# Naming each place of a tile pool: the plan, not the pool, says which place a tile takes

## The chip, the cores and the metric

The kernel runs on one core of a Trainium2 chip. The metric is the time of one execution on the device in microseconds (us); lower is better. The core's engines are TensorE (PE; its weight loads are shown as PEld), VectorE (DVE), ScalarE (ACT), GpSimd (POOL) and SyncE (SP), which issues nearly all transfers. Each runs its own instructions in the order in which they stand, and waits on semaphores for the others.

## The reference

One mixer layer on x of 2048 tokens by 1024 channels: RMS norm, one input projection (2816 columns), two groups of heads side by side (retention in chunks of 128, sliding-window attention of 128 with sinks), gates, one output projection, and x added.

```python
h = rms_norm(x, norm_w).astype(x.dtype)
proj = jnp.einsum('bsd,de->bse', h, w_in).astype(jnp.float32)
rq, rk, rv, rg, sq, sk, sv, sg = jnp.split(proj, offsets, axis=-1)
ro = retention(rotary(rq), rotary(rk), rv)        # scores * decay, state over chunks
ro = group_norm(ro) * ret_norm_w * jax.nn.silu(rg)
so = sliding_window_attention(sq, sk, sv, q_norm_w, k_norm_w, sinks, rel_bias)
so = so * jax.nn.silu(sg)
mixed = jnp.concatenate([ro, so], axis=-1)
x = x + jnp.einsum('bse,ed->bsd', mixed, w_out)
```

## The kernel before, in words

The projections are four products of 2048 tokens, each done as seven half-size products (W2 with its blocks B2, then W1, W3 and W4 in `layer`) over eight pairs of token chunks. Every operand is split into a high and a low part (`split`: ScalarE writes the high part, VectorE the low part), and three matmuls per block multiply the parts. That is the group acc<-w,x of the profile. Sums of blocks (x, w, s, t, u, r) are made on VectorE. Between the products run the window attention (`window`), the retention (`retention`) and the gates (`gate`); their matmuls write tiles named m. What must live longer than SBUF allows goes to DRAM and comes back: sums of blocks to s_dram, projections to aq_dram, rq_dram and g_dram, head outputs to ro_dram and so_dram. Tiles that are transposed by a transfer are first copied by ScalarE (tile apart), stored to planes_dram and read back turned (`turn_by_dma`).

No operation is issued where it is written. `op` records it with what it reads (`r`), writes (`w`) and holds (`also`), a due time and a cost per engine. `Program.emit` then lists them all: at each step it looks at the operations that are ready on every engine, takes the one that can start first by its own clock, allocates its new tiles and issues it. So the source has one line, L421, for all instructions of the profile, and the order on each engine is the plan's. `Order.put` fixes that order for the framework below, which adds the semaphore waits by itself: an instruction that writes a tile waits until the last reader of the tile that lay in the same place has ended.

Places: a working tile (a `Buf` from `kb`) has the tag k, 128 x 512 values, and there are 83 places of it; lg has 4, pT 2, vn 1, and there are 8 banks of PSUM (`CAP`). Small tiles have 3 places per tag unless `COUNTS` says otherwise. The plan keeps for each tag a sorted list of the times at which places come free (`slots`). An operation that needs n places takes the first n entries and starts no earlier than the last of them; when the last user of a tile has been issued, the tile's end by the plan's clock (plus 0.06 us) goes back into the list. For a transfer the plan's end is its time on the bus plus 2.6 us (`dma`).

The list has only times, no places. The place itself comes from `alloc`, which asks the framework's pool for a tile of the tag with so many buffers, and the pool picks one of those that no later instruction in the written order uses any more. Which one it picks, the plan does not say, and the plan's list does not know it.

Of the kernel before, what the change touches and what calls it, by code (L numbers as in the profile page):

```python
# [29 lines left out]
F32 = mybir.dt.float32  # L30
# [9 lines left out]
P = 128  # L40
# [17 lines left out]
BASED = 4  # L58
SUMMED = 4
CAP = {"k": 83, "lg": 4, "pT": 2, "vn": 1, "bank": 8}  # L60
SMALL, COUNTS = 3, {"ms": 1, "rxt": 1, "rqk0t": 1, "rqk1t": 1, "state": 4, "sT": 2}

SHARE = {"x": 11, "raw": 94, "acc": 58, "wr": 31, "wh": 19, "att": 17, "ret": 32, "rin": 87, "gate": 27, "mix": 50, "norm": 16, "res": 7, "turned": 18, "vn": 3, "first": 5, "block": 3, "rest": 6}
# [21 lines left out]
SEM = 0.06  # L85
# [22 lines left out]
def change(a, b):  # L108

    return 0.0 if a == b else LESSER if 0 < a < 3 and 0 < b < 3 else CHANGE  # L110
# [3 lines left out]
class Buf:  # L114


    def __init__(self, tag=None, shape=None, dtype=F32, name="", share=None, ap=None):
        self.tag, self.shape, self.dtype, self.name, self.share = tag, shape, dtype, name, share
        self.ap, self.left, self.end = ap, 0, 0.0
        self.writer, self.readers = None, []  # L120

    def __call__(self):
# [18 lines left out]
class Program:  # L141
# [34 lines left out]
    def emit(self):  # L176
# [2 lines left out]
        free = dict.fromkeys(engines, 0.0)  # L179
        port, table, bus, cut = 0.0, None, 0.0, 0  # L180
        cap = dict(CAP)
        slots = {t: [0.0] * n for t, n in cap.items()}
        used = dict.fromkeys(SHARE, 0)
        count = len(self.ops)
        place, border, asked = 0.0, FIRST, {}
# [19 lines left out]
        while done < count:  # L205
            best = None
            for e, found in avail.items():
                top = None
                base = free[e]
                if e == "T" and not cut:  # L210
                    crowd = sum(o.set in CUTS and o.ready <= base for _, _, o in found[:48])
                for due, n, o in found[:48]:
                    if top is not None and top[0] <= base + 1e-9 and not e == "T":
                        break
                    occ, lat, shared = o.cost[e]
                    s = max(base, o.ready)
                    if e == "T" and o.set:
                        if cut and o.set in CUTS:
                            s = max(base, o.ready + INSIDE)
                            if change(cut, CUTS[o.set]) < CHANGE:  # L220
                                due -= SOONER
                        else:
                            s = max(base, o.ready + SETTLED)
                            if o.set in CUTS:
                                due += LATER - CROWD * min(crowd, MOST)
                    if shared and e != "Q":
                        s = max(s, port)
                    need, short, room = {}, False, 0.0
                    for b in o.new:
                        if b.ap is None:  # L230
                            need.setdefault(b.tag, []).append(b)
                    if any(due > now + AHEAD_OF.get(b.share, 1e9) for b in o.new):
                        continue
                    spare = 0
                    if e == "Q" and need:
                        if due > now + AHEAD:
                            break
                        spare = SPARE
                    for tag, bs in need.items():
                        if tag not in slots:  # L240
                            slots[tag] = [0.0] * COUNTS.get(tag, SMALL)
                        f = slots[tag]
                        if len(f) < len(bs) + (spare if tag == "k" else 0):
                            short = True
                            break
                        room = max(room, f[len(bs) - 1])
                        for share in {b.share for b in bs if b.share}:
                            many = used[share] + sum(b.share == share for b in bs)
                            if many > SHARE[share] - (spare if share in SPARED else 0):
                                short = True  # L250
                    if short:
                        continue
                    s, wait = max(s, room), 0.0
                    if e == "T" and border <= place + o.many:
                        s += late(o, s, occ)
                    if e == "A" and o.set and table and o.set != table:
                        wait = 1.3
                        s += 2.0
                    if top is None or s < top[0] - 1e-9 or (s < top[0] + 1e-9 and due < top[1]):
                        top = (s, due, n, o, wait, room)  # L260
                if top is not None and (best is None or top[:3] < best[0][:3]):
                    best = top, e
            if best is None:
                self.stuck(avail, used, slots)
            (s, _, _, o, wait, room), e = best
            occ, lat, shared = o.cost[e]
            free_before = free[e]
            for e2 in o.cost:
                a = avail[e2]
                a.pop(bisect.bisect_left(a, (o.due, o.n)))  # L270
            for b in o.new:
                if b.ap is None:
                    slots[b.tag].pop(0)
                    if b.share:
                        used[b.share] += 1
                    b.ap = self.alloc(b)
            if e == "Q":
                occ, lat, more = o.cost[e]
                bus = max(bus, s) + occ
                free[e] = max(s + more, bus - BACKLOG)  # L280
                o.end = bus + lat
            else:
                if wait:
                    s = s - 2.0 + wait
                if e == "A" and o.set:
                    table = o.set
                free[e] = s + occ
                o.end = s + lat
                if shared:
                    port = s + occ  # L290
                if e == "T":
                    s = max(free_before, o.ready, room) if o.set else s
                    s += change(cut, CUTS.get(o.set, 0))
                    cut = ENDS.get(o.set, CUTS.get(o.set, 0))
                    s += late(o, s, occ)
                    while border <= place + o.many:
                        border += PIECE
                    a = border - ASKED
                    while a <= place + o.many:
                        asked[a + ASKED] = s + max(a - place, 0) / max(o.many, 1) * occ if a >= place else asked.get(a + ASKED, s)  # L300
                        a += PIECE
                    place += o.many
                    free[e] = s + occ
                    o.end = s + lat
            o.seen = free[e]
            if e == "T" and o.set is None:
                now = max(now, o.due)
            o.go(engines[e])
            done += 1
            if LOG is not None:  # L310
                LOG.append((e, s, free[e], o))
            for b in o.bufs:
                b.left -= 1
                b.end = max(b.end, o.end)
                if not b.left and b.tag:
                    bisect.insort(slots[b.tag], b.end + SEM)
                    if b.share:
                        used[b.share] -= 1
            for d in o.after:
                d.left -= 1  # L320
                same = len(d.cost) == 1 and e in d.cost and e in ("T", "A", "Q") and not o.label.startswith("load")
                t = o.seen if same and e != "Q" else o.end + SEM
                if e == "Q" and now > 0:
                    t += LATE
                if t > d.ready:
                    d.ready, d.by = t, o
                if not d.left:
                    offer(d)
# [96 lines left out]
def layer(ctx, tc, xt, xfirst, xtok, nw, w_in, w_rn, qkw, sinks, biasg, rope, decays, dmask, gpow, w_out, out):  # L425
# [3 lines left out]

    const = ctx.enter_context(tc.tile_pool(name="const", bufs=1))  # L430
    sbuf = ctx.enter_context(tc.tile_pool(name="pool", bufs=1))
    little = ctx.enter_context(tc.tile_pool(name="small", bufs=SMALL))
    psum = ctx.enter_context(tc.tile_pool(name="psum", bufs=1, space=PSUM))
    dram = ctx.enter_context(tc.tile_pool(name="dram", bufs=1, space=DRAM))

    def alloc(b):
        if b.tag == "bank":
            return psum.tile([P, 512], F32, tag=b.tag, bufs=CAP[b.tag], name=b.name)
        if b.tag in ("k", "lg", "pT", "vn"):
            n = {"k": 512, "lg": 640, "pT": 1280, "vn": 1152}[b.tag]  # L440
            return sbuf.tile([P, n], b.dtype, tag=b.tag, bufs=CAP[b.tag], name=b.name)
        return little.tile(b.shape, F32, tag=b.tag, bufs=COUNTS.get(b.tag, SMALL), name=b.name)

    prog = Program(alloc, {"V": V, "G": G, "A": A, "Q": Q, "T": T})
    op = prog.op
# [1258 lines left out]
```

## Time and profile before

| | us |
|---|---|
| median of 3 runs | 674.32 (672.19 to 675.75) |
| profiled execution | 673.73 |
| its span, first to last instruction | 671.9 |
| TensorE busy in the span | 662.2 |
| VectorE busy | 590.2 |
| ScalarE busy | 475.8 |
| transfers: 161.65 MB, mean | 241 GB/s |

The granted TensorE clock is 1.0 throughout. A row of a timeline gives start, duration, engine, line, operation, out<-in, form and count; the bracket at its end is the engine's idle time before it and what ended it. A row of the table of waits gives the waiting engine and tile, what it waited for, the sum in us, how often, and the longest. L421 is the line through which every recorded operation is issued, so groups are told apart by tiles.

### The profile page before, as it was taken

What the parts mean: (1) busy time and instruction counts of PE and PEld (TensorE: products, weight loads), DVE (VectorE), ACT (ScalarE), POOL (GpSimd) and SP (SyncE); (2) the same over time, 40 slices, a digit from 0 to 9 for tenths busy, and PEclk for the clock granted to TensorE, in tenths of its full rate; (3) what the DMA queues carried; (4) which work ended last, traced back from release to release, by engine and by line L of the source; (5) the groups of instructions that cost most, each with busy time, mean ns of one, the idle gap of its engine ahead of it and who ended that gap; (6) DMA issues with size and microseconds to landing.
All of it is one profiled execution on the core that took longest, in us unless ns stands there. A gap on an engine that the chain in (4) does not pass through costs nothing.

```text
span 671.9 us, 16394 instructions
## 1 busy us (share of the span) xinstructions
PE 662.2 (99%) x5956; PEld 562.6 (84%) x5956; DVE 590.2 (88%) x1369; ACT 475.8 (71%) x1154; POOL 15.4 (2%) x39
## 2 busy tenths in 40 slices
PE   9999999999999998999999999999999999999998
PEld 7887888889999998998877787788788888888886
DVE  6998968788699887899989999988999999998762
ACT  7672699657699666887887979999899956343400
POOL 0000000033200000000000000000000000000000
PEclk9999999999999999999999999999999999999999
DMA  9977399979799789999989979989988873447422
GB/s 325 373 222 263 115 353 333 319 241 322 199 275 234 237 254 265 298 291 319 251 197 281 252 208 264 229 252 253 273 293 251 225 212 98 141 115 231 173 94 95
DMA packets 152320, 161.65 MB, mean 241 GB/s; under 512 B 65712, under 2 KB 93232, under 8 KB 152240
## 3 DMA queue, kind: packets, MB, share of 16 engines
q1 hardware_dynamic: 152096, 160.60, 80.2%
q8 instruction: 47, 0.77, 0.5%
q14 instruction: 33, 0.27, 0.1%
q10 hardware_dynamic: 144, 0.00, 0.0%
HBM read 97.58 MB, written 49.35 MB: 219 GB/s over the span
## 4 chain that ended last, share of the span: by engine, by line
PE 82%; DVE 7%; DMA 5%; ACT 4%; issue 1%; SPq 0%; DVEq 0%; ACTq 0%
PE acc L421 74%; PE m L421 8%; DVE x L421 2%; DMA so_dram<-so 2%; ACT ro L421 1%; DMA s_dram<-x 1%; DMA x<-s_dram 1%; DVE lg L421 1%; ACT x L421 1%; DMA g_dram<-c 1%; ACT apart L421 1%; DVE w L421 1%; DVE s L421 1%; ACT qk L421 0%; DVE r L421 0%
## 5 line engine op out<-in xcount | busy, mean ns | idle before, releaser
L421 PE MATMUL acc<-w,x 128*128 128x512 f32 (+1 forms) x2700 | 588.7, 377 | 4.7 <-DVE r L421 1.6
L421 PEld LDWEIGHTS acc<-w,x 128*128 128x128 f32 x2700 | 492.2, 188 | 90.9 <-issue 5.6
L421 DVE TENSOR_TENSOR x<-x 128x512 fp32r<-128x512 f32 (+2 forms) x220 | 144.2, 676 | 24.3 <-ACT x L421 14.4
L421 ACT ACTIVATE x<-x 128x512 fp32r<-128x512 f32 (+1 forms) x187 | 112.1, 619 | 33.8 <-DVE x L421 17.7
L421 DVE TENSOR_TENSOR w<-w 128x512 fp32r<-128x512 f32 (+3 forms) x96 | 60.3, 652 | 0.1
L421 ACT ACTIVATE lg<-lg,nm 128x160 f32<-128x160 f32 x128 | 53.0, 417 | 9.0 <-DVE nm L421 8.8
L421 DVE SCALAR_TENSOR_TENSOR w<-w,nw_sb 128x512 fp32r<-128x512 f32 (+3 forms) x72 | 49.6, 702 | 0.9 <-ACT w L421 0.9
L421 ACT ACTIVATE w<-w 128x512 fp32r<-128x512 f32 (+1 forms) x72 | 40.6, 602 | 11.9 <-DVE w L421 8.0
L421 DVE TENSOR_TENSOR s<-acc,s 128x512 f32<-128x512 f32 (+1 forms) x64 | 41.5, 649 | 6.1 <-PE acc L421 5.8
L421 DVE CUSTOM_DVE_ANT_0 lg<-m,bias,nsnk 128x160 f32<-128x160 f32 x128 | 40.1, 380 | 0.3 <-PE m L421 0.3
L421 DVE TENSOR_TENSOR t<-acc,t 128x512 f32<-128x512 f32 (+2 forms) x33 | 21.1, 639 | 15.3 <-PE acc L421 15.0
L421 ACT ACTIVATE w<-w,nw_sb 128x512 fp32r<-128x512 f32 (+3 forms) x43 | 27.5, 682 | 3.1 <-DMA w<-in_w_in 2.4
L421 ACT ACTIVATE s<-acc 128x512 f32<-128x512 f32 (+1 forms) x32 | 18.0, 566 | 14.2 <-PE acc L421 13.6
L421 ACT ACTIVATE ro<-ro,nmu,rg 128x128 f32<-128x128 f32 x64 | 25.1, 481 | 2.7 <-DVE nmu L421 2.6
L421 DVE STREAM_TRANSPOSE pT<-lg 128x640 f32<-128x640 f32 x32 | 25.6, 821 | 0.0
L421 DVE TENSOR_TENSOR r<-acc,t 128x512 f32<-128x512 f32 (+1 forms) x32 | 20.8, 650 | 5.2 <-PE acc L421 5.1
L421 ACT ACTIVATE x<-go 128x512 fp32r<-128x512 f32 x28 | 17.5, 631 | 10.5 <-PE acc L421 6.8
L421 ACT ACTIVATION_READ_ACCUMULATOR lg<-lg,nm 128x1 f32 x128 | 24.2, 189 | 0.0
L421 DVE TENSOR_TENSOR t<-acc,s 128x512 f32<-128x512 f32 (+1 forms) x32 | 20.7, 648 | 3.1 <-PE acc L421 2.5
L421 ACT ACTIVATE apart<-qn 128x1024 uint16<-128x1024 uint16 x16 | 16.9, 1065 | 7.6 <-DVE qn L421 7.1
L421 PE MATMUL m<-pT,vn 32*64 32x128 f32 (+1 forms) x1152 | 21.0, 286 | 0.3 <-DVE state L421 0.2
L421 ACT ACTIVATE ro<-m 64x256 f32<-64x256 f32 (+2 forms) x53 | 20.8, 396 | 0.6
(144 smaller groups left out, 591.1 us busy)
## 6 DMA issues: line engine op xcount, KB each, us to landing
x<-in_xt SPq DMA_DIRECT2D x80, 256.0 KB, 4.8
planes_dram<-apart SPq DMA_DIRECT2D x52, 256.0 KB, 3.6
x<-s_dram SPq DMA_DIRECT2D x48, 256.0 KB, 4.2
w<-in_w_in SPq DMA_DIRECT2D x40, 256.0 KB, 5.2
xk<-in_xtok SPq DMA_DIRECT2D x32, 256.0 KB, 5.1
res<-in_xtok SPq DMA_DIRECT2D x32, 256.0 KB, 3.8
s_dram<-x SPq DMA_DIRECT2D x24, 256.0 KB, 3.9
w<-in_w_out SPq DMA_DIRECT2D x20, 256.0 KB, 5.6
```

Source lines behind the costliest of these rows:

```text
L421: return lambda *a, **k: self.order.put(op(*a, **k))
```

## The change

A place gets a number. The plan's lists hold pairs (time, number) in place of times, an operation that takes an entry notes its number in the tile (`Buf.slot`), and the number goes back into the list with the tile's end. `alloc` makes the tag out of the kind and the number (k17, bank3), with one buffer each, so the tile lies in the place that the plan took from the head of its list. The counts stay: 83 places of k, 8 banks and so on. The times in the lists are as before, so every choice of the plan is too.

```diff
 CAP = {"k": 83, "lg": 4, "pT": 2, "vn": 1, "bank": 8}
+WIDE = {"k": 512, "lg": 640, "pT": 1280, "vn": 1152}
...
-        self.ap, self.left, self.end = ap, 0, 0.0
+        self.ap, self.left, self.end, self.slot = ap, 0, 0.0, None
...
-        slots = {t: [0.0] * n for t, n in cap.items()}
+        slots = {t: [(0.0, i) for i in range(n)] for t, n in cap.items()}
...
-                            slots[tag] = [0.0] * COUNTS.get(tag, SMALL)
+                            slots[tag] = [(0.0, i) for i in range(COUNTS.get(tag, SMALL))]
...
-                        room = max(room, f[len(bs) - 1])
+                        room = max(room, f[len(bs) - 1][0])
...
-                    slots[b.tag].pop(0)
+                    b.slot = slots[b.tag].pop(0)[1]
...
-                    bisect.insort(slots[b.tag], b.end + SEM)
+                    bisect.insort(slots[b.tag], (b.end + SEM, b.slot))
...
-    little = ctx.enter_context(tc.tile_pool(name="small", bufs=SMALL))
+    little = ctx.enter_context(tc.tile_pool(name="small", bufs=1))
...
     def alloc(b):
+        tag = f"{b.tag}{b.slot}"
         if b.tag == "bank":
-            return psum.tile([P, 512], F32, tag=b.tag, bufs=CAP[b.tag], name=b.name)
-        if b.tag in ("k", "lg", "pT", "vn"):
-            n = {"k": 512, "lg": 640, "pT": 1280, "vn": 1152}[b.tag]
-            return sbuf.tile([P, n], b.dtype, tag=b.tag, bufs=CAP[b.tag], name=b.name)
-        return little.tile(b.shape, F32, tag=b.tag, bufs=COUNTS.get(b.tag, SMALL), name=b.name)
+            return psum.tile([P, 512], F32, tag=tag, name=b.name)
+        if b.tag in WIDE:
+            return sbuf.tile([P, WIDE[b.tag]], b.dtype, tag=tag, name=b.name)
+        return little.tile(b.shape, F32, tag=tag, name=b.name)
```

No instruction moves on any engine. What differs is the waits, which the order prints in brackets by the engine or transfer semaphore waited for (DMAHW0 to DMAHW7 count the landings of SP's transfers, loads and stores alike). The number at a tile's name only tells tiles apart. Three places follow, each before and after; the line number is one higher after the change because of the line added.

VectorE in the first product (sums of blocks, 52 to 58 us in the profile), before and after:

```order
L421 TENSOR_TENSOR s_265<-acc_671,s_265 128x512 [waits PE_49]
L421 TENSOR_TENSOR x_715<-x_572,x_631 128x512 [waits DMAHW6_49]
L421 TENSOR_TENSOR x_721<-x_641,x_651 128x512 [waits DMAHW1_49,DMAHW0_49,DVE_49]
L421 TENSOR_TENSOR x_726<-x_715,x_240 128x512 [waits DMAHW4_49,DVE_49]
L421 TENSOR_TENSOR x_572<-x_240,x_572 128x512
L421 TENSOR_TENSOR s_284<-acc_705,s_284 128x512 [waits PE_49]
L421 TENSOR_TENSOR x_745<-x_721,x_250 128x512 [waits DMAHW5_49,DVE_49]
```

```order
L422 TENSOR_TENSOR s_265<-acc_671,s_265 128x512 [waits PE_49]
L422 TENSOR_TENSOR x_715<-x_572,x_631 128x512 [waits DMAHW6_49,DMAHW4_49]
L422 TENSOR_TENSOR x_721<-x_641,x_651 128x512 [waits DMAHW1_49,DMAHW0_49]
L422 TENSOR_TENSOR x_726<-x_715,x_240 128x512 [waits DVE_49]
L422 TENSOR_TENSOR x_572<-x_240,x_572 128x512 [waits DMAHW5_49]
L422 TENSOR_TENSOR s_284<-acc_705,s_284 128x512 [waits PE_49]
L422 TENSOR_TENSOR x_745<-x_721,x_250 128x512 [waits DMAHW4_49,DVE_49]
```

x_726 (at 55.81 in the profile) loses its wait on a transfer; x_745 (57.62) now waits on the semaphore that x_726 waited on.

ScalarE between the first and the second product (164 to 171 us), before and after. The x are high parts of blocks, c and s copies out of the accumulators, apart the copy ahead of a transpose:

```order
L421 ACTIVATE c_2006<-acc_1902 128x384 [waits PE_49]
L421 ACTIVATE x_2011<-x_1637 128x512 [waits DMAHW3_49]
L421 ACTIVATE x_2021<-x_1648 128x512 [waits DMAHW4_49,DVE_49]
L421 ACTIVATE c_2032<-acc_1936 128x384 [waits DMAHW5_49,PE_49]
L421 ACTIVATE ks_120<-m_2024,wqk_76 128x256 [waits PE_49]
L421 ACTIVATE apart_2045<-qn_2014 128x1024 [waits DVE_49]
L421 ACTIVATE x_2058<-x_1659 128x512 [waits DMAHW7_49,DVE_49]
L421 ACTIVATE s_2065<-acc_2027 128x384 [waits DMAHW0_49,PE_49]
```

```order
L422 ACTIVATE c_2006<-acc_1902 128x384 [waits PE_49]
L422 ACTIVATE x_2011<-x_1637 128x512 [waits DMAHW3_49,DVE_49]
L422 ACTIVATE x_2021<-x_1648 128x512 [waits DMAHW4_49,DMAHW2_49]
L422 ACTIVATE c_2032<-acc_1936 128x384 [waits PE_49]
L422 ACTIVATE ks_120<-m_2024,wqk_76 128x256 [waits PE_49]
L422 ACTIVATE apart_2045<-qn_2014 128x1024 [waits DVE_49]
L422 ACTIVATE x_2058<-x_1659 128x512 [waits DMAHW5_49]
L422 ACTIVATE s_2065<-acc_2027 128x384 [waits PE_49]
```

c_2032 and s_2065 (at 168.03 and 170.84) lose a wait on a transfer, x_2011 (165.47) gains one on VectorE, and x_2021 changes VectorE for a transfer.

ScalarE in the second product, around the attention (247 to 254 us), before and after:

```order
L421 ACTIVATE x_3494<-x_2850 128x512 [waits DMAHW7_49,DVE_49]
L421 ACTIVATE apart_3501<-qn_3483 128x1024 [waits DVE_49,PE_49]
L421 ACTIVATE x_3513<-x_2869 128x512 [waits DMAHW5_49,Activation_49]
L421 ACTIVATE x_3533<-x_2889 128x512 [waits DMAHW3_49,Activation_49]
L421 ACTIVATE ks_2144<-m_3539,wqk_76 128x128 [waits PE_49]
```

```order
L422 ACTIVATE x_3494<-x_2850 128x512 [waits DMAHW7_49,DMAHW3_49]
L422 ACTIVATE apart_3501<-qn_3483 128x1024 [waits DVE_49,PE_49]
L422 ACTIVATE x_3513<-x_2869 128x512 [waits DVE_49]
L422 ACTIVATE x_3533<-x_2889 128x512 [waits PE_49]
L422 ACTIVATE ks_2144<-m_3539,wqk_76 128x128 [waits PE_49]
```

x_3513 (at 252.91) and x_3533 exchange a transfer for VectorE and TensorE.

## The prediction

> **What bounds the kernel now.** I read the page first (busy shares, then the chain that ended last), then the table of waits, then the timelines of TensorE's weight loads and of the engines that feed it.
>
> ```profile
> PE 662.2 (99%) x5956; PEld 562.6 (84%) x5956; DVE 590.2 (88%) x1369; ACT 475.8 (71%) x1154; POOL 15.4 (2%) x39
> PE 82%; DVE 7%; DMA 5%; ACT 4%; issue 1%; SPq 0%; DVEq 0%; ACTq 0%
> L421 PEld LDWEIGHTS acc<-w,x 128*128 128x128 f32 x2700 | 492.2, 188 | 90.9 <-issue 5.6
> ```
>
> TensorE is the bound, but 17% of the chain that ended last runs through VectorE, ScalarE and transfers: there TensorE stood still. A matmul's end is modelled, so I measure those stalls on the weight loads (PEld). Between two loads of one product 90.9 / 2700 = 0.03 us of idle is ordinary; more is a stall. The timeline of PEld shows these (the bracket is the idle time before the row and what ended it):
>
> ```profile
> 66.17 1.92 PEld L421 LDWEIGHTS acc<-w,x 128*128 128x128 f32 x9 [1.22 <-DVE x L421]
> 171.38 0.47 PEld L421 LDWEIGHTS acc<-w,x 128*128 128x128 f32 x3 [0.27 <-ACT s L421]
> 255.39 0.47 PEld L421 LDWEIGHTS acc<-w,x 128*128 128x128 f32 x3 [0.99 <-DVE r L421]
> 372.73 0.50 PEld L421 LDWEIGHTS m<-v,sT 64*64 64x64 f32 x14 [0.74 <-DVE sT L421]
> 377.87 2.59 PEld L421 LDWEIGHTS acc<-w,x 128*128 128x128 f32 x12 [0.48 <-ACT ro L421]
> 380.81 0.43 PEld L421 LDWEIGHTS m<-v,sT 64*64 64x64 f32 x16 [0.35 <-DVE s L421]
> 419.67 0.30 PEld L421 LDWEIGHTS acc<-w,x 128*128 128x128 f32 x2 [0.17 <-issue]
> 427.47 0.53 PEld L421 LDWEIGHTS acc<-w,x 128*128 128x128 f32 x3 [0.60 <-DVE t L421]
> 431.53 0.53 PEld L421 LDWEIGHTS acc<-w,x 128*128 128x128 f32 x3 [0.84 <-PE m L421]
> 483.13 1.92 PEld L421 LDWEIGHTS acc<-w,x 128*128 128x128 f32 x9 [1.17 <-DVE r L421]
> ```
>
> The rows at 380.81 and 419.67 show what a change of matmul form costs anyway: 0.35 before m<-v,sT, 0.17 before acc after m. Less the ordinary part, the stalls are 1.19 (66.17), 0.24 (171.38), 0.96 (255.39), 0.39 (372.73), 0.45 (377.87), 0.43 (427.47), 0.81 (431.53) and 1.14 (483.13): 5.6 us.
>
> Who makes the feeders late? The table of waits has rows in which a compute engine waits for a store to DRAM:
>
> ```profile
> ACT so L421 <- DMA planes_dram<-apart: 4.4, 2, 2.3
> ACT x L421 <- DMA so_dram<-so: 3.5, 1, 3.5
> ACT apart L421 <- DMA planes_dram<-apart: 1.6, 2, 0.8
> DVE x L421 <- DMA so_dram<-so: 2.6, 1, 2.6
> DVE x L421 <- DMA planes_dram<-apart: 2.2, 1, 2.2
> DVE x L421 <- DMA s_dram<-x: 2.0, 1, 2.0
> ```
>
> The writers of x, so and apart take nothing from a finished store. What they wait for is the place: their tile was put where the stored tile lay, and the store must have read it. These six rows hold 16.3 us of VectorE and ScalarE time. Following each stall back on the timelines, four groups of stalls end in such a wait (the sixth row here is from the chain of waits):
>
> ```profile
> 55.81 1.29 DVE L421 TENSOR_TENSOR x<-x 128x512 f32<-128x512 f32 x2 [2.03 <-DMA s_dram<-x]
> 57.62 0.68 DVE L421 TENSOR_TENSOR x<-x 128x512 f32<-128x512 f32 x1
> 165.86 0.82 DVE L421 TENSOR_TENSOR x<-x 128x512 fp32r<-128x512 f32 x1 [2.16 <-DMA planes_dram<-apart]
> 170.84 0.49 ACT L421 ACTIVATE s<-acc 128x384 f32<-128x384 f32 x1 [0.48 <-DMA planes_dram<-apart]
> 248.39 1.06 ACT L421 ACTIVATE apart<-qn 128x1024 uint16<-128x1024 uint16 x1
> 246.81 6.02 DMA so_dram<-so
> 252.91 1.15 ACT L421 ACTIVATE x<-x 128x512 fp32r<-128x512 f32 x2 [3.47 <-DMA so_dram<-so]
> 370.58 0.69 DVE L421 TENSOR_TENSOR x<-x 128x512 fp32r<-128x512 f32 x1 [2.63 <-DMA so_dram<-so]
> 418.84 1.06 ACT L421 ACTIVATE apart<-qk 128x1024 uint16<-128x1024 uint16 x1 [0.81 <-DMA planes_dram<-apart]
> ```
>
> **The change part by part.** Instructions, operands and order are as before; tags and the list of pairs cost nothing on the chip. What moves is who had a tile's place before it, so waits. The plan keys the free places by its own estimate of their end, which counts a store's landing (2.6 us after the bus); before, the pool handed out places without that estimate. Hence I expect a place that a store still reads to be passed over for one that is free. The order printed above shows it at 55.81, 170.84 and 252.91, and it is the same at 370.58 and 418.84: the wait on a transfer is gone, and what is left is an engine's result that is ready or nearly so.
>
> *66.17.* VectorE runs without a gap from 55.81 to 66.1, so 2.03 us of it come earlier; but the transfer's semaphore is now named by the add at 57.62, 57.62 - 55.81 = 1.81 us further down the line, so up to 1.81 of the wait is saved. The stall is 1.19: all of it goes, if the landing stays; I take 1.1.
>
> *171.38.* ScalarE's s<-acc no longer waits 0.48: 0.2 goes (the whole stall).
>
> *255.39.* ScalarE's x<-x waited 3.47, VectorE waited for it and TensorE for VectorE: 0.96 goes.
>
> *372.73 and 377.87.* VectorE's 2.63 covers 0.39 + 0.45 = 0.8.
>
> *427.47 and 431.53.* ScalarE's 0.81 at 418.84 is smaller than the two stalls (1.24), and each engine can gain no more than the wait that fed it: 0.8.
>
> *483.13* has no store behind it: stays.
>
> Gains: 1.1 + 0.2 + 0.96 + 0.8 + 0.8 = 3.9 us.
>
> Against this stand new waits. The plan's end of a tile can be too early, and an in-order engine is then held with all that is behind it. The largest that I find on ScalarE, with the VectorE or TensorE row that it now has to wait for:
>
> ```profile
> 165.47 0.62 ACT L421 ACTIVATE x<-x 128x512 fp32r<-128x512 f32 x1
> 332.30 0.69 ACT L421 ACTIVATE x<-x 128x512 fp32r<-128x512 f32 x1
> 333.70 0.42 DVE L421 TENSOR_TENSOR qk<-tsin,tcos 128x256 f32<-128x256 f32 x1
> 393.27 1.14 ACT L421 ACTIVATE w<-w 128x512 fp32r<-128x512 f32 x2
> 394.47 0.68 DVE L421 TENSOR_TENSOR x<-x 128x512 fp32r<-128x512 f32 x1
> 427.68 1.14 ACT L421 ACTIVATE x<-x 128x512 fp32r<-128x512 f32 x2
> 427.42 0.68 DVE L421 TENSOR_TENSOR w<-w 128x512 fp32r<-128x512 f32 x1
> 571.34 0.63 ACT L421 ACTIVATE x<-x 128x512 fp32r<-128x512 f32 x1 [0.31 <-DVE x L421]
> 569.63 4.60 PE L421 MATMUL acc<-w,x 128*128 128x512 f32 x19
> ```
>
> At 165.47 the awaited x<-x ends at 165.86 + 0.82 = 166.68: 1.2 late. At 332.30: 334.12, 1.8. At 393.27: 395.15, 1.9. At 427.68: 428.10, 0.4. At 571.34 it is a matmul of the run that ends at 574.23: 2.9 at most. Sum 8.2. Queued behind them are ScalarE's next splits and copies out of the accumulators, and TensorE waits for those. Their price lies between 0 (ScalarE is 71% busy, so a late start can be caught up; VectorE's wait of 2.16 at 165.86, with which 165.47 is tied, is itself a store's) and 8.2. I take 0.4: the one at 427.68 stands straight behind a stall, the others have ScalarE idle time after them. Net 3.9 - 0.4 = 3.5.
>
> How late is a store? Here 6.02 us from issue to landing. The Trainium skill, page "DMA: Bandwidth & Descriptors", section "Anatomy of one DMA", states about 2.0 us plus bytes / 436 GB/s; 256 KB would take an estimated 2.6, so the store of 246.81 would have landed at 249.4, when ScalarE came free (248.39 + 1.06), and the sum without that term would be 2.5. The trace does not agree at this spot, and its 6.02 decides.
>
> The profiled execution took 673.73 us, 671.9 of span and 1.8 around it, and is 0.6 below the median of 674.32 (runs 672.19 to 675.75). 673.73 - 3.5 = 670.2; I take **670.2 us**, 0.6% below the median. Shifts of 0.5% (3.4 us: below 670.9, above 677.7) are about what a measurement of this kernel can tell from no change.
>
> **The rivals.** *A, the shortage moves on.* There are as many places as before, so a place that a store holds late goes to another tile and its writer waits instead, as the add at 57.62 does. For it: that wait, and transfers that fill the engines in places, so that a load issued earlier need not land earlier:
>
> ```profile
> 370.00:380.00 10.00, 9.56 (x97) 7.49 (x96) 8.82 (x25) 9.23 (x24) 0.00 (x0) 1.00 1.14 287
> ```
>
> (the last but one column: the sixteen DMA engines' share, 1.14). Against it: at the other four spots no store is named. No gain, 0.4 of loss: 674.1. The Trainium skill's rule on consistent bubbles ("Perfetto Trace Analysis", "Optimization Strategy": they can mean too few buffers) points this way; the bubbles here are eight single ones, mostly far apart, so the trace hardly bears it out.
>
> *B, ScalarE behind places still in use* (slower). The new waits of 8.2 reach TensorE instead of being caught up; decided once more than 3.9 of them do. All of them: 673.73 - 3.9 + 8.2 = 678.0. For it: VectorE, which most of these wait for, is 88% busy. Against: ScalarE's 71%.
>
> *C, more than the sum.* The same rule frees SP's queue and the loads come earlier, and 483.13 and the rest of 431.53 go too: 673.73 - 5.6 = 668.1.
>
> *D, nothing changes* in who follows whom: ruled out by the printed order.
>
> **How the numbers follow.** Forecast 0.60, its own range 668.7 (all 3.9 and more, no loss) to 672.3 (only the two waits far longer than their stalls, 0.96 + 0.8, less 0.4): 0.47 faster, 0.13 same. A 0.15: 0.13 same, 0.02 slower. B 0.12: slower. C 0.13: faster. So faster 0.60, same 0.26, slower 0.14. The range from 666.5 (all of C, with the runs' scatter) to 675.5 leaves out most of B.
>
> **What would show it.** Right: PEld without the idle time at 66, 255, 372 and 427; VectorE and ScalarE waits on stores far below 16 us in the table of waits; 483 still there. ScalarE waiting a microsecond or more near 165, 332 or 393 without a stall of PEld behind it would show the losses caught up. Wrong: waits on stores as large as before on other tiles (A), or new idle time of PEld ended by ACT x or ACT s near 395 to 400 or 575 to 600 (B).

## The result, and the profile after

| | before | after |
|---|---|---|
| median of six runs each, taken together | 672.8 us (671.73 to 675.75) | 667.63 us (666.95 to 668.84) |
| ratio, with its 95% interval | | 0.992 (0.9897 to 0.9942) |
| profiled execution | 673.73 us | 668.84 us |
| its span | 671.9 us | 667.1 us |

The change makes the kernel 0.8% faster, 4.8 us in the two profiled spans. After the change, the busy times, the chain that ended last, and the group of the products' weight loads are these.

```profile
PE 661.0 (99%) x5956; PEld 563.2 (84%) x5956; DVE 591.1 (89%) x1369; ACT 478.3 (72%) x1154; POOL 16.1 (2%) x39
PE 92%; DVE 3%; ACT 2%; DMA 1%; issue 1%; SPq 0%; ACTq 0%
L422 PEld LDWEIGHTS acc<-w,x 128*128 128x128 f32 x2700 | 492.9, 188 | 85.8 <-issue 4.3
```

VectorE and ScalarE are busy 0.9 and 2.5 us longer than before, so it isn't their work that shrank. What went is TensorE's standing still: the chain runs through TensorE for 92% of its length instead of 82%, and the idle time of this one group fell from 90.9 to 85.8 us, by itself 5.1 us. The table of waits, rows in which a compute engine waits for a store, after the change (all of them):

```profile
ACT apart L422 <- DMA planes_dram<-apart: 0.8, 1, 0.8
ACT x L422 <- DMA aq_dram<-t: 0.8, 1, 0.8
ACT w L422 <- DMA rq_dram<-t: 0.6, 1, 0.6
ACT x L422 <- DMA planes_dram<-apart: 0.6, 1, 0.6
DVE qn L422 <- DMA planes_dram<-apart: 1.9, 1, 1.9
```

That is 4.7 us. Before, all such rows together (the six quoted in the prediction and eleven smaller ones) made 13.7 us on ScalarE and 11.3 on VectorE. The timeline of TensorE's weight loads after the change, at the places of the eight stalls:

```profile
63.95 4.04 PEld L422 LDWEIGHTS acc<-w,x 128*128 128x128 f32 x18
...
166.36 8.30 PEld L422 LDWEIGHTS acc<-w,x 128*128 128x128 f32 x48
...
253.91 1.75 PEld L422 LDWEIGHTS acc<-w,x 128*128 128x128 f32 x10
...
271.64 0.92 PEld L422 LDWEIGHTS m<-pT,vn 32*64 32x64 f32 x58 [0.85 <-issue]
...
369.48 0.43 PEld L422 LDWEIGHTS m<-v,sT 64*64 64x64 f32 x16 [0.35 <-DVE st L422]
...
374.05 2.59 PEld L422 LDWEIGHTS acc<-w,x 128*128 128x128 f32 x12
...
422.89 2.59 PEld L422 LDWEIGHTS acc<-w,x 128*128 128x128 f32 x12 [0.17 <-issue]
...
426.34 1.68 PEld L422 LDWEIGHTS acc<-w,x 128*128 128x128 f32 x8 [0.23 <-issue]
...
478.21 6.90 PEld L422 LDWEIGHTS acc<-w,x 128*128 128x128 f32 x31 [1.15 <-DVE r L422]
```

Rows without a bracket have no idle time ahead of them: the stalls of 66, 171, 255 and 377 are gone, 372 and 427 have only the ordinary 0.35 and 0.17 of a change of form, 431 has 0.23 left of 0.84 (now at 426.34), and the one of 483 stands as it was, now at 478. The row at 271.64 is new (see the last section).

Both programs issue the same 5,956 weight loads in the same order, so the start of load k can be set against that of load k before. The difference changes in steps. At 66.17 the program gains 1.18 us and at 69.18 another 0.38, at 171.38 0.29, at 255.39 1.00, at 265.02 1.20, at 360.35 0.51, at 372.73 0.39, at 377.87 0.39, at 405.47 0.27, at 427.47 0.43, at 431.53 0.61. It loses 0.73 in the first 6 us, 0.50 (net) at 273 to 274 and 0.29 at 437. Together with the small steps that is 4.85 us.

### The profile page after: what moved, and what is told of

The parts are those of the page before. It is cut to its first block, busy times and chain, and to the rows that moved or that the text cites. A ratio compares the mean times of both kernels' runs of the same rounds, so it can differ in the third digit from the quotient of the medians.

```text
span 667.1 us, 16311 instructions
## 1 busy us (share of the span) xinstructions
PE 661.0 (99%) x5956; PEld 563.2 (84%) x5956; DVE 591.1 (89%) x1369; ACT 478.3 (72%) x1154; POOL 16.1 (2%) x39
## 4 chain that ended last, share of the span: by engine, by line
PE 92%; DVE 3%; ACT 2%; DMA 1%; issue 1%; SPq 0%; ACTq 0%
PE acc L422 82%; PE m L422 10%; ACT ro L422 1%; DMA r<-planes_dram 1%; DVE lg L422 1%; DMA v<-aq_dram 1%; DVE w L422 0%; DVE x L422 0%; SPq L422 0%; ACT x L422 0%; DVE t L422 0%; DVE st L422 0%; DVE ro L422 0%; ACT s L422 0%; DVE go L422 0%
## 5 line engine op out<-in xcount | busy, mean ns | idle before, releaser
L422 PEld LDWEIGHTS acc<-w,x 128*128 128x128 f32 x2700 | 492.9, 188 | 85.8 <-issue 4.3
L422 ACT ACTIVATE x<-x 128x512 fp32r<-128x512 f32 (+1 forms) x187 | 112.9, 621 | 29.6 <-PE acc L422 15.2
L422 ACT ACTIVATE s<-acc 128x512 f32<-128x512 f32 (+1 forms) x32 | 18.0, 565 | 13.7 <-PE acc L422 13.5
L422 PEld LDWEIGHTS m<-pT,vn 32*64 32x64 f32 x1152 | 18.5, 130 | 2.7 <-issue 2.1
```

Source lines behind the costliest of these rows:

```text
L422: return lambda *a, **k: self.order.put(op(*a, **k))
```

## The experiments

All kernels have the same instructions in the same order as before and after; only the places of tiles differ. The time of the kernel before, measured beside them, was 673.8 us (e1 to e4, 17 runs), 673.63 (e5 to e8, 18 runs) and 673.1 (e9 to e11, 12 runs). In most of them the plan keeps its list of times as it is, and the number of the place comes from a second list, `spots`, with a key of its own.

**Which places?** e1 names only the k, e2 all but the k:

```diff
 def alloc(b):
+        named = b.tag == "k"
+        tag, n = (f"{b.tag}{b.slot}", 1) if named else (b.tag, CAP.get(b.tag, COUNTS.get(b.tag, SMALL)))
...
-            return sbuf.tile([P, WIDE[b.tag]], b.dtype, tag=tag, name=b.name)
+            return sbuf.tile([P, WIDE[b.tag]], b.dtype, tag=tag, bufs=n, name=b.name)
```

> Only the 83 places of k are named by the plan; banks, lg, pT, vn and the small tiles are handed out by the pool as before. Theory 1 (the gain is store waits, and only tiles of k share places with stored tiles): all of the gain, 667.6 us, ratio 0.992, and ScalarE's and VectorE's waits on stores about 4 us as after the change. Rival 2 (the banks' or the small tiles' choice brings it): 672.8 us, ratio 1.000.

> The converse of e1: banks, lg, pT, vn and the small tiles are named by the plan, k is handed out by the pool as before. Theory 1: no change, 672.8 us, ratio 1.000, waits of ScalarE and VectorE on stores about 25 us as before. Rival 2: 667.6 us.

Measured: e1 667.25 us, ratio 0.9895 (0.9865 to 0.9926), waits of the two engines on stores 4.3 us; e2 672.44 us, 0.9989 (0.9963 to 1.0016), 22.7 us. The whole gain lies in the choice of the k. e2 still has the rows that e1 lost; the largest of each engine in its table of waits:

```profile
ACT x L422 <- DMA so_dram<-so: 2.0, 1, 2.0
...
DVE x L422 <- DMA so_dram<-so: 2.5, 1, 2.5
```

**Is it the name, or the choice?** e3 names the places of k and hands them out in the written order; e4 keeps the plan's key, but without the landing:

```diff
+                b.stored = e == "Q" if o.end > b.end else b.stored
...
                     bisect.insort(slots[b.tag], (b.end + SEM, b.slot))
+                    bisect.insort(spots[b.tag], (done, b.slot))                             # e3
+                    bisect.insort(spots[b.tag], (b.end + (PAD if b.stored else 0), b.slot))  # e4, PAD = -2.6
```

> Places of k are named, with one tag each, but handed out in the written order: the place whose last user was issued first goes first, with no estimate of an end; the rest as before. Theory 1: the gain is gone; 672.8 us if the pool's own pick is about the written order, and slower than before if the pool knows more than that. Rival 3 (a tag for each place is worth something in itself, whatever the choice): 667.6 us.

> As after the change, but a place whose last user is a transfer is sorted into the list of numbers by its end less 2.6 us, that is without the landing; the list of times, so every choice of the plan, is unchanged. Theory 1 (what counts is that the landing of stores is in the key): the waits of ScalarE and VectorE on stores come back to 25 us or more, and the time to 672.8 us or above, ratio 1.000 to 1.010. Rival 4 (what counts is the order in which the engines free places): 667.6 us, ratio 0.992, waits on stores near 4 us.

Measured: e3 705.12 us, 1.0453 (1.0417 to 1.0488); e4 682.67 us, 1.0125 (1.0086 to 1.0164), a little above its forecast. A name is worth nothing by itself, and leaving 2.6 us out of one key costs 15 us against e1. The waits on stores are 49.4 us in e3 and 29.6 in e4. In e3 they reach TensorE in single long stalls; the timeline of PEld in e3:

```profile
62.50 4.87 PEld L428 LDWEIGHTS acc<-w,x 128*128 128x128 f32 x22 [2.06 <-DVE x L428]
...
172.51 6.43 PEld L428 LDWEIGHTS acc<-w,x 128*128 128x128 f32 x24 [6.30 <-ACT s L428]
...
341.24 0.78 PEld L428 LDWEIGHTS acc<-w,x 128*128 128x128 f32 x3 [2.69 <-ACT s L428]
```

That e3 is 31 us slower than before also shows that the pool did not go by the written order: its own pick was much better than that. By what rule it picks, no run shows. Not all of the 31 us is standing still: TensorE is also busy 12.8 us longer in e3 (675.0 against 662.2), in part because its granted clock fell after some of the stalls (last section).

**Who must not stand behind a store?** In e5 compute engines choose without the landing and loads with it; in e6 the other way round:

```diff
+                    blind = e != "Q"        # e5;  e == "Q" in e6
+                    spot = min(spots[b.tag], key=lambda p: (p[blind], p[2]))
...
+                    spots[b.tag].append((b.end, b.end - (2.6 if b.stored else 0), b.slot))
```

> All places named. An operation of a compute engine picks the place that the plan's list of ends without the landing of transfers puts first (as in e4); a load picks by the ends with the landing (as after the change). Theory 1a (stores cost time because ScalarE and VectorE stand behind them): as e4 or near it, 677 to 683 us, waits of ScalarE and VectorE on stores 25 us or more. Rival 5 (they cost time because loads into such places hold SP's queue, and with it all later loads): 667 to 669 us, waits of SP on stores near the 8.1 us of after.

> The converse of e5: loads pick by the ends without the landing, compute engines by the ends with it. Theory 1a: no loss, 667 to 668 us, waits of ScalarE and VectorE on stores below 4 us, those of SP on stores well above 8 us. Rival 5: 677 to 683 us.

Measured: e5 678.31 us, 1.0073 (1.0047 to 1.0099); e6 668.43 us, 0.993 (0.9906 to 0.9955). The compute engines are the ones that pay: in e5 they wait 33.0 us for stores and SP 3.4. In e6 SP waits 47.0 us for stores (8.6 after the change, where the 8.1 of the expectations leaves out two small rows, and 23.8 before), and the time is within 1.2 us of e1, e8 and e11 (667.25 to 667.67). e4, where loads and compute engines both choose blind, is 4.4 us slower than e5, although its compute engines wait less (29.6 us); whether SP's 27.6 us of waits cost something there, no run separates. From e6, the largest of SP's rows, and the only three of compute engines:

```profile
SPq L431 <- DMA planes_dram<-apart: 26.8, 22, 4.5
SPq L431 <- DMA aq_dram<-t: 4.4, 5, 1.8
...
ACT w L431 <- DMA planes_dram<-apart: 0.8, 1, 0.8
ACT x L431 <- DMA ro_dram<-ro: 0.7, 1, 0.7
ACT x L431 <- DMA rq_dram<-r: 0.3, 1, 0.3
```

**Stores alone, and how late?** e7 has e3's written order with the places of stores put back by 40 operations; e8 has the change's key with 1.5 us more for a store:

```diff
+                    bisect.insort(spots[b.tag], (done + (BACK if b.stored else 0), b.slot))  # e7, BACK = 40
+                    bisect.insort(spots[b.tag], (b.end + (PAD if b.stored else 0), b.slot))   # e8, PAD = 1.5
```

> As e3 (places of k in the written order of their release), but a place whose last user is a transfer is put back as if it had been released 40 operations later, some 7 us at 6 operations per us. No end by the plan's clock is used. Theory 1 (only the stores matter): 667 to 669 us, waits of ScalarE and VectorE on stores below 4 us. Rival 4 (the plan's ends of the engines' own users matter too): 673 us or more, with ScalarE or VectorE waiting for one another where they did not.

> As after the change, but a place whose last user is a transfer is sorted into the list of numbers by its end plus 1.5 us, since the stores seen on the chip land some 4 us or more after the bus rather than 2.6. Theory 1: the waits of ScalarE and VectorE on stores that were left (4.7 us) fall to about 2, and as hardly any of them reached TensorE the time stays at 667 us, at best 0.5 us below e1. Rival 6 (what is left of the chain outside TensorE is still store waits): 665 us or below.

Measured: e7 669.14 us, 0.9946 (0.9926 to 0.9967), with 1.2 us of waits on stores; e8 667.25 us, 0.9917 (0.9892 to 0.9942), with 2.4. From e3 to e7, by moving nothing but the places of stores, 36 us come back. What the plan's ends of engine users add is about the 1.9 us between e7 and e8 at most; e7's profiled execution also has a stall of 1.55 us without a wait (last section), so it may be less. e8 does as expected: less waiting on stores, the same time. The waits left after the change cost nothing that these runs can tell, and no version here beats e1 and e8.

**Single spots.** e9 and e10 put three tiles each back into the place that they had before, each that of one stored tile (`BACK` holds the numbers of the two tiles in the order of allocation; the tiles allocated later take the heads of the list as it then stands):

```diff
+BACK = {171: 149, 771: 763, 1152: 1138}        # e9;  {1021: 1007, 1141: 1130, 1675: 1668} in e10
...
+                    k = [i for _, i in f].index(lay[BACK[given]]) if given in BACK else 0
+                    b.slot = f.pop(k)[1]
```

> As after the change, but three tiles are put back where they lay before it, each in the place of a stored tile: VectorE's x behind the store at 55.81 (2.03 us of wait before), ScalarE's x at 252.91 (3.47) and VectorE's x at 370.58 (2.63): 8.1 us of waits, all at spots from which the prediction follows a stall of TensorE. Theory 1: their terms come back, 1.1 + 0.96 + 0.8 = 2.9 us, so 670.5 us, with PEld's stalls at 66, 255 and 372 to 378 and none at 171 and 427. Rival 7 (it is the sum of the waits that counts, wherever they stand: 25 us of them cost 4.8 us of span): 1.6 us, 669.2 us.

> As e9 with three other tiles, all of ScalarE: so at 328.63 (2.14 us of wait before), so at 365.86 (1.59) and so at 542.11 (2.31): 6.0 us of waits, with no stall of TensorE followed back to them. Theory 1: nothing, 667.6 us, no new stall of PEld over 0.3 us. Rival 7: 1.2 us, 668.8 us.

> The changed kernel once more, as the reference of e9 and e10 in the same call: 667.6 us. Stalls of PEld that no wait explains (issue, 0 to 1.7 us near 265 to 272) may stand elsewhere; the rest as in the trace of after.

Measured: e11 667.67 us, 0.9913 (0.9893 to 0.9934); e9 669.79 us, 0.9952 (0.993 to 0.9973); e10 667.48 us, 0.9909 (0.9887 to 0.9932). e10 loses nothing. e9 loses 2.1 us (its runs, 668.9 to 670.9, all lie above those of e11, 666.43 to 668.21). That is between the two forecasts (2.9 and 1.6), so e9 by itself doesn't decide between theory 1 and rival 7; e10 does. The profiled execution of e9, 668.9 us, is the fastest of its seven, and it shows what it paid for. ScalarE, VectorE and PEld in e9:

```profile
55.97 1.89 DVE L432 TENSOR_TENSOR x<-x 128x512 f32<-128x512 f32 x3
...
251.02 1.16 ACT L432 ACTIVATE x<-x 128x512 fp32r<-128x512 f32 x2 [2.75 <-DMA so_dram<-so]
...
253.50 2.06 PEld L432 LDWEIGHTS acc<-w,x 128*128 128x128 f32 x12 [0.32 <-DVE r L432]
...
366.17 0.69 DVE L432 TENSOR_TENSOR x<-x 128x512 fp32r<-128x512 f32 x1 [2.80 <-ACT apart L432]
...
373.45 2.59 PEld L432 LDWEIGHTS acc<-w,x 128*128 128x128 f32 x12 [0.45 <-ACT ro L432]
...
426.46 2.57 PEld L432 LDWEIGHTS acc<-w,x 128*128 128x128 f32 x12 [0.58 <-PE m L432]
```

At the first spot the store had landed in time in this execution, so there is no wait and no stall (in the slower ones it may have been there); at the second the wait is 0.7 shorter than before and the stall 0.32 instead of 0.99; at the third (the row names ScalarE's apart, which ends at the same moment as the landing of the store issued at 361.35, after 4.9 us; after the change the same x runs at 364.81, before that apart begins at 366.28, so it doesn't need it) the stall of 377 is back and that of 372 isn't. Two waits of nearly 3 us thus cost TensorE a third of a microsecond at one spot and, as the last row shows, more than one at the other.

The last row, 426.46, is the stall of 431 before, and it hangs on the third spot too. Against e10, which has no such wait there, the x starts 1.58 us later (366.17; e10 364.59), though e9 had been 0.12 ahead until then. From 370 to beyond 430 VectorE and ScalarE both run 1.1 us later than in e10. TensorE falls back to them in three steps: 0.36 at 373.45, 0.27 at 401.06 and 0.52 at 426.46, together 1.15. The same three come back in e12, below, whose only edit in common with e9 is this tile.

In e10's trace the waits put back are 6.2 us: 5.5 for planes_dram at two spots, and 0.74 for g_dram at the third, where 1.59 stood before. Why the two large ones cost nothing is another matter than slack. ScalarE's so in after, then the same tile in e10:

```profile
326.64 1.47 ACT L422 ACTIVATE so<-m 128x128 f32<-128x128 f32 x8 [2.60 <-issue]
...
537.60 1.47 ACT L422 ACTIVATE so<-m 128x128 f32<-128x128 f32 x8 [2.62 <-DVE ro L422]
```

```profile
325.99 1.47 ACT L432 ACTIVATE so<-m 128x128 f32<-128x128 f32 x8 [2.96 <-DMA planes_dram<-apart]
...
536.59 1.47 ACT L432 ACTIVATE so<-m 128x128 f32<-128x128 f32 x8 [2.54 <-DMA planes_dram<-apart]
```

Without the store ScalarE stands just as long for something else: the store was the last of several releasers, by little. The Trainium skill ("Perfetto Trace Analysis", section "Optimization Strategy") says to find a gap's blocker by the semaphore that it waits for and the instruction that updates it. For e9's spots that rule gives the right answer; for these two rows the runs show that the blocker's successor must be asked for as well.

**Two waits in a row.** In the chain of before the store behind VectorE's wait at 370.58 was itself issued late, after ScalarE's wait at 365.86. e12 is e9's edit with `BACK = {1141: 1130, 1152: 1138}`:

> As after the change, with two tiles put back that follow one another in the chain of before: ScalarE's so (365.86 before) in the place that the store to g_dram reads, and VectorE's x (370.58) in the place that the store of so reads, which was issued behind that so. Theory 8 (the stall at 372 and 377 is two store waits in a row): x waits 2.6 us or more for the store to so_dram and PEld stalls by 0.8 us at 368 to 374, against 0.42 in e9, where x alone was put back. Rival 9 (the first wait adds nothing, as in e10): as e9, 0.4 us.

Measured, in a single run: 668.7 us. The chain of e12, start, length and what:

```profile
356.17 3.45 DMA g_dram<-c
...
359.65 0.05 ACT so L432
...
361.04 4.83 DMA so_dram<-so
...
365.99 0.10 DVE x L432
```

The links are those of before, but the store to g_dram landed early enough to hold ScalarE 0.30 us only. VectorE's x waited 3.27 us, and PEld stalled 0.46 at 373.27, as in e9 (0.45). So the chain exists, and whether its first wait adds to the stall stays open, as it was hardly there.

## Why the prediction was right, and where not

Forecast were 670.2 us and 3.5 us off the profiled execution; measured are 667.63 us and 4.8 off the span. The direction, the mechanism and the rule were right; the size was too small.

- *A place that a store still reads is passed over.* Right, and it is the whole gain: e1 against e2 for the tiles, e4 and e7 for the store's landing as the part of the key that counts. Of the pool, which by the prediction chose "without that estimate", the runs show only that it chose worse than the plan does, not by what rule.
- *66.17, taken at 1.1.* Measured 1.18, and 0.38 at 69.18, which was not in the list of stalls. e9 didn't bring the wait at 55.81 back, but four traces have it, at four lengths:

  | | VectorE's wait for the store to s_dram | stall of PEld at 66.17 | at 69.18 |
  |---|---|---|---|
  | before | 2.03 | 1.22 | 0.41 |
  | e5 | 1.87 | 1.07 | 0.42 |
  | e4 | 1.68 | 0.87 | 0.42 |
  | e2 | 0.99 | 0.18 | 0.41 |
  | after, e1, e6 to e12 | none | 0.04 | 0.04 |

  The first stall is the wait less 0.8 in all four: so much could VectorE be late here for nothing, and all beyond it reached TensorE. The second stands as soon as there is a wait of this kind. (e3's VectorE waits elsewhere in that stretch.) The wait that moved to the add at 57.62 cost nothing: after the change VectorE runs through that stretch without a bracket.
- *171.38 at 0.2, 255.39 at 0.96, 372.73 and 377.87 at 0.8.* Measured 0.29, 1.00 and 0.78. The causes at 255 and 377 were shown by e9, which brought back a third of the one and nearly all of the other. That of 372 was not shown, nor that of 171: in e2 the same ScalarE copy waits 0.76 for a store, and there is no stall there (TensorE had stood 0.46 us a little earlier).
- *427.47 and 431.53 at 0.8.* Measured 0.43 and 0.61, more than ScalarE's wait of 0.81 can feed. For 431 the step is wrong: in e9 and e12 its stall is back (0.58) although ScalarE's apart (418.84 before) waits for no store there, and e2 has 0.61 without that wait too. By e9 it hangs on VectorE's wait at 370.58, 61 us ahead, which was credited with 372 and 377 alone; so does the 0.27 at 405.47, which was in no list. For 427, which stays at 0.17 in e9, e12 and e2, the step to ScalarE's 0.81 is neither shown nor refuted.
- *483.13 stays.* Right: 1.15 in the row at 478.21. Rival C, near in time, needed it gone, and needed SP's freed queue to bring loads earlier: SP's waits on stores did fall from 23.8 to 8.6 us, but e6, with 47.0, is at most 1.2 us slower than e1, e8 and e11.
- *New ScalarE waits, up to 8.2, taken at 0.4.* At the named places after the change:

```profile
164.86 0.63 ACT L422 ACTIVATE x<-x 128x512 fp32r<-128x512 f32 x1
...
330.53 0.63 ACT L422 ACTIVATE x<-x 128x512 fp32r<-128x512 f32 x1
...
390.66 1.15 ACT L422 ACTIVATE w<-w 128x512 fp32r<-128x512 f32 x2 [0.92 <-DVE x L422]
...
422.95 1.16 ACT L422 ACTIVATE x<-x 128x512 fp32r<-128x512 f32 x2 [0.22 <-DVE w L422]
...
568.51 0.63 ACT L422 ACTIVATE x<-x 128x512 fp32r<-128x512 f32 x1 [1.95 <-PE acc L422]
```

  These are 0, 0, 0.92, 0.22 and 1.95: 3.1 us, and no stall of PEld is shown to come of them. The one small new idle time that ends with ScalarE, 0.18 at 432.60 (the 0.29 lost at 437), isn't in e11, the same kernel, which has the same 0.22. So the price was about 0 rather than 0.4. At 165.86 the bound was too high because the awaited VectorE instruction comes earlier by the same change (its own 2.16 is gone); for the others the reason isn't shown. Rival B falls.
- *Rival A, the shortage moves on.* It falls for compute engines (25.0 to 4.7 us). e6 shows where the shortage may go: to loads, for which SP can wait 47 us.

The step that failed in size is the sum of the gains: 3.9 forecast, and 4.94 measured at the same waits (1.56 + 0.29 + 1.00 + 0.78 + 0.27 + 1.04). The list of stalls was made by looking for large brackets on PEld and left out small ones that hang on the same late engine. It also left out, without a reason, the 1.19 at 265.02 that ends with `issue`. That 4.94 lies so near to the 4.85 of the spans is luck: the stalls without a wait around 265 to 274 gave 0.70 net, the first 6 us took 0.73, and neither has to do with the change as far as the runs show. The rest are 0.51 gained at 360.35, also ahead of a row that ends with `issue`, 0.29 lost at 437, and 0.28 lost in small steps.

The median moved more than the profile (672.8 to 667.63, and 6.5 us beside e1): the profiled execution is one of several, and the times of before scatter more, which fits a kernel that waits for landings. Its 17 runs beside e1 lie between 671.25 and 679.52, those of e1 between 666.12 and 668.17.

## What to carry to other kernels

Where a planner hands out buffers as here, let it choose the place too, by the time at which the last reader is really done, a store's landing included; a compute engine is to be given a place that no store reads, and loads may take the others if the queue that issues them has time. Before pricing a wait in a table of waits, look for what would release that instruction next: a store that was the last of several releasers by some tenths of a microsecond cost nothing here, while three that held an engine for 2.0 to 3.5 us cost 1.0 to 1.7 each, all their stalls counted. When stalls are listed for a sum, follow each late engine forward to all the stalls behind it, the small ones as well: here VectorE and ScalarE, which feed each other and had hardly any idle time left, stayed late for 60 us.

## What the hardware showed beside that

**Landings.** A store to so_dram took 6.02 us to land at 246.81 before, and stores of the same size (256 KB) 4.83 in e12's chain and 4.9 in e9. By the Trainium skill ("DMA: Bandwidth & Descriptors", section "Anatomy of one DMA"), about 2.0 us and the bytes at 436 GB/s, an estimate would be 2.6. None of these three rows agrees with it; but the section gives that sum for transfers issued through GpSimd, and these are issued by SP, so they don't test it. The medians from issue to landing, bus included, are 3.6 us for the 52 stores to planes_dram and 3.9 for the 24 to s_dram before.

**The clock after a long stall.** In e3, after TensorE had stood 6.30 us (up to 172.51), its granted clock was 0.50 from 171 to 177 and 0.85 from 177 to 179, and 24 loads took 6.43 us where the next 24 took 4.14. After the stall of 2.69 up to 341.24 it was 0.61 and then 0.54 until 345. It was low once more, 0.57 from 512 to 516, behind a stall of 1.34. e4 and e5 have the same stall of 1.34 before the same load, and e4 one of 2.33, and in neither is a stretch of 4 us below 0.99 but the last; so the length of a single stall doesn't decide it, and what does, no run shows.

**Stalls without a wait.** Before, PEld stands 1.19 us at 265.02 before a load for which the profile names no wait; after, 0.85 us at 271.64; in e2 and e7 it is the rows below, in e4 1.04 at 362.83 and in e3 0.65 at 342.67, and e1, e5, e6, e8, e9, e10 and e12 have none over 0.42.

```profile
264.73 2.03 PEld L422 LDWEIGHTS acc<-w,x 128*128 128x128 f32 x12 [1.72 <-issue]
```

```profile
272.56 0.93 PEld L429 LDWEIGHTS m<-pT,vn 32*64 32x64 f32 x60 [1.55 <-issue]
```

Most stand at 265 to 273 or near 360 and come and go; e11, the same kernel as after, has 0.58 at 271.41. A likely cause can be read from the traces. The third section of a page lists 47 transfers of 16 KB, of kind instruction, on queue q8. Counting TensorE's 5,956 loads in their order, one of these transfers lands at load 2122 in before and 2124 in e2, and the stall stands at that very load; in the other twelve traces it lands at 2117 or earlier, and there is none. The next lands at 2242, 2247 and 2214 in after, e7 and e11, which stall at 2247 or 2249, and at 2196 or earlier in the other eleven, which don't. The five stalls end 1.2 to 1.8 us behind the landing. So TensorE seems to have run out of instructions there. As no run moves such a transfer on purpose, this is argued, not shown. A single profiled span is uncertain by about as much: after has 667.1 and e11 666.4 us.
